# Grouped-query attention scores: the second product of each score tile over 128 stacked rows instead of 64

## The chip, the cores and the metric

The kernel runs on one core of a Trainium2 chip. The metric is the device time of one execution in microseconds. Three runs of the kernel before took 1809.95, 1822.38 and 1826.61 us, median 1822.38 us.

## What is computed

A two-layer trunk works on 256 context tokens and 256 latent tokens of width 1024. Each layer has a feed-forward half step, a mixing sub-layer and a second feed-forward half step. In the mixing sub-layer one input projection is split among three groups: A (a recurrent matrix memory, mLSTM), B (attention with low-rank compression) and C (windowed grouped-query attention). The change touches group C alone, which is cut here to what it needs:

```python
def gqa_branch(...):          # 6 query heads, 2 key heads, head width 64
    q = rms_norm(q, q_norm); k = rms_norm(k, k_norm)      # latent tokens also get a rotary embedding
    s_band = einsum(qb, kb) * C_SCALE                      # latent queries, latent keys within 128 tokens
    s_ctx  = einsum(qb, k_c) * C_SCALE                     # latent queries, all context keys
    p = softmax(concat([s_sink, s_ctx, s_band]))           # a learned sink logit per head
    o = p[ctx] @ v_c + p[band] @ v_band
    # where need_ctx (layer 0 only): the same for the 256 context queries over the context keys, without a band
```

## The kernel before, in words

All weights and activations are fp32. A large product is made as three products of rounded halves: the rounded high part (type fp32r) of each operand, and the rest (the low part). `mm3` (L234) issues high by high, low by high and high by low into one PSUM tile.

The scores of group C do the same with two products, by stacking. `u_q` (L908) writes the query transposed and twice: `twice` (L870) transposes a tile that holds each head's 64 columns two times, so that partitions 0 to 63 and 64 to 127 of the PSUM tile both hold the head. L937 rounds all 128 partitions into `qTC`, and L938 replaces partitions 64 to 127 by what the rounding took off. So one stationary operand of 128 rows holds the query's high part on top and its low part below. `u_k2` (L874) does it for the key: L897 writes the rounded high part on all 128 partitions (`kh`, the first half of `kTC`), and L898 writes what the rounding took off, the low part `kl`, on partitions 0 to 63 alone.

`attend` (L600) makes a tile of 128 queries by `nk` keys for one head (`nk` is 256 in the context stream s=0, 512 in the latent stream s=1). For C the list `prods` (L612) has two products, issued at L614 through `mm` (L231, so every one of them stands under line L232 in the profile, as `sc<-big,w`): the stacked query (128 rows) by `kh`, then the query's upper 64 rows by `kl`. In the latent stream a third product adds the mask (L617, `sc<-maskn,ident`). Then come the row maximum (L625, VectorE), the exponential (L630, ScalarE), the normalisation (L639 or L641), the transposes (L647, TensorE), their copies (L653) and, for two heads together, the product with the values (L661, TensorE, 64 columns of the array each).

There are 36 such tiles in an execution: 12 in the context stream and 12 in the latent stream of layer 0, and 12 in the latent stream of layer 1 (there the context stream is no longer needed). They are not issued in one piece. `mix` (L1161) makes a list of units of work (projections, tiles of B and C, heads of the mLSTM), sorts them by the table `PLAN`, and `run` (L189) steps several of them in turn, so that a tile's steps lie between steps of other units. The framework's scheduler then sets the final order of the instructions of each engine. Each engine runs its own instructions in order and waits at an instruction whose input is not there.

In the layer-0 mix the C tiles run from 536 us to 638 us of the span, in the layer-1 mix from 1519 us to 1573 us. Behind each mix come the output projection (`u_wout`, L1132) and the next feed-forward step.

Of the kernel before, what the change touches and what calls it, by code (L numbers as in the profile page):

```python
# [10 lines left out]
F32 = mybir.dt.float32  # L11
F32R = mybir.dt.float32r
AF = mybir.ActivationFunctionType
ALU = mybir.AluOpType
# [21 lines left out]
def dper(nj):  # L36
    return {2: 4, 3: 2, 4: 2}.get(nj, 1)


# PLAN: order of the units of work of a mix layer, as (first place, step) per group of units.  # L40
# CFG: units taken up per round, units under way at once.  CHP: halves of a weight chunk whose low part Pool makes.
# OPT: engine of a copy or product where it is not the usual one.  BANK, BANKS: PSUM pool by use, and the exceptions.
# MODS: tiles of the next norm made after each column tile of the last group.
PLAN = [
# [11 lines left out]
CFG = [(2, 9), (1, 10)]  # L56
CHP = [
    {"k1": 1, "cq": 1, "o": 1, "k2": 0, "v": 1, "q1": 1, "q2": 1},
    {"k1": 1, "cq": 0, "o": 1, "k2": 0, "v": 0, "q1": 0, "q2": 1},
]  # L60
# [10 lines left out]
BANK = {"k1tr": "tr", "pk": "sc", "pvv": "sc", "cqtr": "tr", "pq": "sc", "k2tr": "tr", "qtr": "tr", "gtr": "tr",  # L71
# [3 lines left out]
BANKS = [  # L75
    {"k1tr": "sc", "C": "ps", "hT": "hold"},
    {"ms": "ps", "ftr": "sc", "hT": "sc"},
    {},
]
MODS = {0: (0, 0, 0, 2, 1, 1, 0, 0), 2: (0, 0, 0, 1, 1, 1, 1, 1), 3: (0, 0, 0, 2, 1, 1, 0, 0)}  # L80


def group(key):
    if isinstance(key, str):
        return key
    if key[0] in "BC":
        return f"{key[0]}{key[1]}{key[2]}"
    if key[0] in ("m", "w", "fin"):
        return f"{key[0]}{key[1]}"
    if key[0] in ("k1", "k2"):  # L90
        return f"{key[0]}{key[1] // 2}"
    return key[0]
# [46 lines left out]
class Builder:  # L139
# [734 lines left out]
    def u_k2(self, l, tt, getps):  # L874
        nc = self.nc
        self.phase = f"K2_{l}"
        lat = 1 if tt >= 2 else 0
        u = slice(tt * P, (tt + 1) * P)
        ps = getps()
        yield  # L880
        self.phase = f"K2_{l}"
        self.cp("VC", self.VC[:, tt, :], ps[:, P:2 * P])
        qk = self.a2([P, 2, 64])
        self.cp("k2", qk, ps[:, 0:P].rearrange("p (a b) -> p a b", a=2))
        qd = self.a2([P, 2, 2, 64])
        yield from self.qknorm(qk, 2, 64, None if lat else qd)
        if lat:
            self.rope(qk, 2, 32, self.tabs_c[tt - 2], 1, qd)
        yield
        self.phase = f"K2_{l}"  # L890
        tr = self.ps((P, 2, P), "k2tr")
        self.twice(tr, qd)
        yield
        self.phase = f"K2_{l}"
        g = self.ones if lat else self.gcol[:, 8:9]
        kh, kl = self.kTC
        self.cp("kh", kh[:, :, u], tr, g)  # L897
        nc.vector.scalar_tensor_tensor(kl[0:64, :, u], tr[0:64], g[0:64], kh.bitcast(F32)[0:64, :, u],  # L898
                                       op0=ALU.mult, op1=ALU.subtract)

    def u_v(self, l, tt, getps):
        self.phase = f"v_{l}"
# [258 lines left out]
    def mix(self, l, need, pre, nxt):  # L1161
        nc = self.nc
# [42 lines left out]
        units = k1[:2] + [("n1", self.u_norm(n1), set())] + k2[:2] + k1[2:] + k2[2:]  # L1205
# [10 lines left out]
        def att(kind, s, hp):  # L1216
            if kind == "B":
                heads = (2 * hp, 2 * hp + 1)
                t = self.attend(f"attB{l}{s}", s, heads, lambda hd, tt: [self.qTB[:, hd, tt * P:(tt + 1) * P]],
                                lambda hd, nk: [self.kTB[:, hd, 0:nk]],  # L1220
                                lambda kt, hd: self.VB[:, kt, hd * 64:hd * 64 + 64], self.y[2 + hp])
                kn, qn = "k1", "cq"
            else:
                def qT(hd, tt):
                    q = self.qTC[hd % 3][:, hd // 3, tt * P:(tt + 1) * P]
                    return q, q[0:64]

                def kT(hd, nk):
                    return self.kTC[0][:, hd // 3, 0:nk], self.kTC[1][0:64, hd // 3, 0:nk]

                t = self.attend(f"attC{l}{s}", s, (hp, hp + 3), qT, kT,
                                lambda kt, hd: self.VC[:, kt, 64 * (hd // 3):64 * (hd // 3) + 64],
                                self.y[5 + hp], masked=True, sink=self.sink)
                kn, qn = "k2", "q1" if hp < 2 else "q2"
            return [((kind, s, hp, k), g, {(kn, tt) for tt in range(2 * s + 2)} | {(qn, 2 * s + k % 2)})
                    for k, g in enumerate(t)]
# [8 lines left out]
        for s in streams:  # L1245
            tiles = [t for u in (("C", 0), ("B", 2), ("C", 1), ("C", 2)) for t in att(u[0], s, u[1])]
# [24 lines left out]
        for u in units:  # L1271
            g = group(u[0])
# [162 lines left out]
```

## Time and profile before

| what | value |
|---|---|
| median of three runs | 1822.38 us |
| the three runs | 1809.95, 1822.38, 1826.61 us |
| profiled execution, span from first to last instruction | 1810.0 us |
| mean granted TensorE clock of the profiled execution | 0.989 |

The profiled execution's span of 1810.0 us is as long as the shortest of the three runs (1809.95 us) and 12.4 us shorter than their median. In the rows below PE is TensorE's matmul, PEld its weight load, DVE VectorE, ACT ScalarE, POOL GpSimd. A matmul's row gives its start and how long it took. Matmuls are pipelined: a row begins while the one before it still drains, so what a matmul costs a busy TensorE is the distance from the end of the one before to its own end, and not its own length. In the shape of a matmul, `64*128 64x512` is a stationary operand of 64 rows and 128 columns and a moving operand of 64 rows and 512 columns.

### The profile page before, as it was taken

The numbers are of one execution on the slowest core, as the hardware profiler recorded it, in microseconds if no ns is written. First come the engines' busy times: TensorE is split into PE (matmuls) and PEld (weight loads), VectorE is DVE, ScalarE is ACT, GpSimd is POOL, SyncE is SP. The second block draws the span as 40 slices with busy tenths as digits, with TensorE's granted clock in tenths as the row PEclk, the third lists the DMA queues.
The fourth block names the chain that finished last, engine by engine and source line by source line (L and its number), as shares of the span: only waits on it lengthen the run. The fifth ranks groups of instructions, "written<-read, shape, count | busy, mean of one in ns | idle before, by whom it ended". The sixth has DMA issues, their size and how long they took to land. (4 is left out here: it accounts for less than half of the span.)

```text
span 1810.0 us, 27331 instructions
## 1 busy us (share of the span) xinstructions
PE 1763.1 (97%) x10098; PEld 1500.9 (83%) x10098; DVE 1235.3 (68%) x2795; ACT 704.3 (39%) x1334; POOL 353.9 (20%) x364
## 2 busy tenths in 40 slices
PE   7999999999999999999999999999999999999999
PEld 5787888889876789888888898888888886699998
DVE  4799698947777766986853469885334788645555
ACT  3422222235565554322322352222222665544443
POOL 2320221035354572000000030000000555340000
PEclk9999999999998999999999999999999999899999
DMA  8656455622110136564533346654223231035654
GB/s 329 206 173 226 148 187 185 210 91 102 36 36 24 48 113 202 189 218 145 199 111 93 119 137 209 212 161 148 79 80 119 68 118 48 12 117 168 205 158 146
DMA packets 99591, 252.35 MB, mean 139 GB/s; under 512 B 12289, under 2 KB 16769, under 8 KB 98433
## 3 DMA queue, kind: packets, MB, share of 16 engines
q1 hardware_dynamic: 99456, 250.60, 42.5%
q8 instruction: 79, 1.29, 0.3%
q14 instruction: 56, 0.45, 0.1%
HBM read 249.51 MB, written 1.05 MB: 138 GB/s over the span
## 5 line engine op out<-in xcount | busy, mean ns | idle before, releaser
L243 ACT ACTIVATE w<-raw 128x1024 fp32r<-128x1024 f32 (+2 forms) x366 | 344.6, 943 | 550.1 <-PE ps L232 277.6
L247 DVE TENSOR_TENSOR w<-raw,w 128x1024 fp32r<-128x1024 f32 (+1 forms) x310 | 333.1, 1075 | 188.0 <-ACT w L243 186.4
L232 PE MATMUL sc<-h,w 128*128 128x512 f32 (+1 forms) x1152 | 303.8, 373 | 0.2 <-DVE h L380 0.2
L232 PE MATMUL tr<-h,w 128*128 128x512 f32 (+1 forms) x1128 | 295.6, 372 | 1.2 <-ACT h L379 0.8
L232 PE MATMUL sc<-big,w 128*128 128x256 f32 (+3 forms) x1200 | 275.4, 337 | 1.7 <-ACT big L379 1.1
L245 POOL TENSOR_TENSOR w<-raw,w 128x1024 fp32r<-128x1024 f32 (+2 forms) x56 | 138.5, 2475 | 652.8 <-ACT w L243 638.5
L232 PE MATMUL ps<-h,w 128*128 128x256 f32 (+1 forms) x1680 | 259.8, 314 | 2.3 <-DVE x L429 2.0
L232 PEld LDWEIGHTS ps<-h,w 128*128 128x128 f32 x1680 | 236.0, 190 | 23.1 <-DVE x L429 2.6
L232 PE MATMUL ps<-big,w 128*128 128x512 f32 (+1 forms) x1152 | 247.3, 374 | 7.8 <-DVE x L429 4.9
L232 PEld LDWEIGHTS ps<-big,w 128*128 128x128 f32 x1152 | 205.3, 189 | 48.0 <-DVE x L429 6.1
L232 PE MATMUL tr<-big,w 128*128 128x256 f32 (+1 forms) x1128 | 243.7, 327 | 0.0
L232 PEld LDWEIGHTS sc<-h,w 128*128 128x128 f32 x1152 | 207.1, 189 | 39.6 <-issue 1.6
L232 PEld LDWEIGHTS tr<-h,w 128*128 128x128 f32 x1128 | 202.9, 189 | 38.5 <-ACT h L379 1.0
L232 PEld LDWEIGHTS sc<-big,w 128*128 128x128 f32 (+1 forms) x1200 | 197.0, 192 | 30.4 <-issue 9.1
L232 PEld LDWEIGHTS tr<-big,w 128*128 128x128 f32 x1128 | 183.0, 192 | 17.8
L345 DVE CUSTOM_DVE_ANT_0 a<-a,a 128x512 f32<-128x512 f32 x256 | 190.3, 743 | 4.3
L345 DVE CUSTOM_DVE_ANT_0 hold<-a,a 128x512 f32<-128x512 f32 x256 | 182.2, 712 | 11.4 <-DMA a<-ada_t 11.2
L232 PE MATMUL ps<-w,h 128*128 128x256 f32 (+1 forms) x1152 | 164.6, 296 | 5.0 <-ACT h L868 2.5
L232 PEld LDWEIGHTS ps<-w,h 128*128 128x128 f32 x1152 | 148.3, 192 | 11.6 <-ACT h L868 2.7
L429 DVE SCALAR_TENSOR_TENSOR x<-ps,gate,x 128x256 f32<-128x256 f32 x192 | 87.3, 480 | 94.5 <-PE ps L232 94.2
L460 DVE TENSOR_TENSOR a<-a,tr 128x512 f32<-128x512 f32 (+1 forms) x90 | 54.3, 603 | 141.6 <-PE tr L232 70.4
L459 ACT ACTIVATE a<-sc 128x512 f32<-128x512 f32 (+1 forms) x91 | 48.3, 531 | 259.7 <-PE sc L232 245.1
(249 smaller groups left out, 1587.1 us busy)
## 6 DMA issues: line engine op xcount, KB each, us to landing
raw<-wi SPq DMA_DIRECT2D x176, 512.0 KB, 4.2
a<-ada_t SPq DMA_DIRECT2D x256, 256.0 KB, 4.7
raw<-wo SPq DMA_DIRECT2D x128, 320.0 KB, 3.0
raw<-w_out SPq DMA_DIRECT2D x24, 512.0 KB, 3.4
big<-ada_s SPq DMA_DIRECT2D x8, 1024.0 KB, 10.9
raw<-wo SPq DMA_DIRECT2D x8, 512.0 KB, 3.7
raw<-win_q SPq DMA_DIRECT2D x8, 512.0 KB, 3.8
a<-crow SPq DMA_DIRECT2D x12, 256.0 KB, 5.7
```

The lines of the kernel that those rows point to most:

```text
L232: self.nc.tensor.matmul(out, lhsT, rhs, start=start, stop=stop)
L243: nc.scalar.activation(h, raw, AF.Copy)
L245: nc.gpsimd.tensor_tensor(l, raw, h.bitcast(F32), op=ALU.subtract)
L247: nc.vector.tensor_tensor(l, raw, h.bitcast(F32), op=ALU.subtract)
L345: nc.vector.tensor_tensor_reduce(out=w if s else junk, in0=w, in1=self.cb[s, hf], scale=1.0, scalar=0.0, op0=ALU.mult, op1=ALU.add, accum_ ...
L429: self.nc.vector.scalar_tensor_tensor(xs, ps, self.gate[l][:, s, i, d:d + 1], xs, op0=ALU.mult, op1=ALU.add)
L459: nc.scalar.activation(sg, pg, AF.Silu)
L460: nc.vector.tensor_tensor(sg, sg, pu, op=ALU.mult)
```

## The change

The low part of the key is written on all 128 partitions, and the second product takes the whole stacked query (128 rows) and the low part of the key on 128 rows. It adds one small term, low by low, to the scores.

```diff
         kh, kl = self.kTC
         self.cp("kh", kh[:, :, u], tr, g)
-        nc.vector.scalar_tensor_tensor(kl[0:64, :, u], tr[0:64], g[0:64], kh.bitcast(F32)[0:64, :, u],
-                                       op0=ALU.mult, op1=ALU.subtract)
+        nc.vector.scalar_tensor_tensor(kl[:, :, u], tr, g, kh.bitcast(F32)[:, :, u], op0=ALU.mult, op1=ALU.subtract)
...
                 def qT(hd, tt):
                     q = self.qTC[hd % 3][:, hd // 3, tt * P:(tt + 1) * P]
-                    return q, q[0:64]
+                    return q, q
 
                 def kT(hd, nk):
-                    return self.kTC[0][:, hd // 3, 0:nk], self.kTC[1][0:64, hd // 3, 0:nk]
+                    return self.kTC[0][:, hd // 3, 0:nk], self.kTC[1][:, hd // 3, 0:nk]
```

Comments above `PLAN` are dropped as well. No instruction is added, removed or moved: each engine has the same instructions in the same order before and after, the DMA queues too. What differs is the shape of 36 matmuls with their weight loads (64 rows become 128) and of eight VectorE instructions of L898 (64 partitions become 128).

## Rows read from the trace of the kernel before

**Rows 1.** The profile page: busy us of each engine, share of the span, instructions.
```profile
PE 1763.1 (97%) x10098; PEld 1500.9 (83%) x10098; DVE 1235.3 (68%) x2795; ACT 704.3 (39%) x1334; POOL 353.9 (20%) x364
```

**Rows 2.** Busy time by stretch, in us; the first line names the columns.
```profile
core 0: us, PE busy (x) PEld busy (x) DVE busy (x) ACT busy (x) POOL busy (x), PEclk, DMA share, GB/s
537.00:552.00 15.00, 12.76 (x93) 10.37 (x94) 11.60 (x26) 8.64 (x28) 8.03 (x8) 1.00 0.15 40
553.52:563.76 10.24, 10.24 (x37) 6.98 (x36) 6.09 (x24) 4.80 (x16) 3.21 (x10) 0.50 0.01 2
564.00:640.00 76.00, 76.00 (x486) 54.55 (x486) 57.68 (x196) 45.74 (x143) 39.32 (x64) 1.00 0.11 36
1548.00:1573.00 25.00, 24.65 (x102) 15.77 (x101) 15.60 (x55) 12.71 (x39) 5.91 (x12) 0.80 0.01 1
```

**Rows 3.** What TensorE waited for, us in total, times, longest: 530:645, then 1500:1585.
```profile
PE sc L1052 <- DVE big L221: 2.2, 1, 2.2
...
PE ps L661 <- DVE a L221: 1.1, 3, 0.6
```

**Rows 4.** The chain that ended last, within 1515:1590: start us, us, what.
```profile
1519.77 0.93 PE sc L232 x3
...
1523.05 3.41 DVE a L1020 x4
...
1567.71 2.09 PE sc L232 x6
...
1573.95 1.48 DVE sa L636
```

**Rows 5.** Groups by line and shape: the 64-row products.
```profile
L232 PE MATMUL sc<-big,w 64*128 64x512 f32 x24 | 12.2, 510 | 0.0
L232 PE MATMUL sc<-big,w 64*128 64x256 f32 x12 | 4.8, 398 | 0.0
```

**Rows 6.** Timeline of TensorE at one latent tile: start us, us, what.
```profile
584.65 0.47 PE L232 MATMUL sc<-big,w 128*128 128x512 f32 x1
...
585.06 0.50 PE L232 MATMUL sc<-big,w 64*128 64x512 f32 x1
...
585.49 0.33 PE L232 MATMUL sc<-maskn,ident 128*128 128x128 f32 x1
```

**Rows 7.** Timeline of TensorE: full products behind one another.
```profile
120.22 0.84 PE L232 MATMUL tr<-h,w 128*128 128x512 f32 x3
120.90 0.84 PE L232 MATMUL sc<-h,w 128*128 128x512 f32 x3
...
665.79 5.88 PE L232 MATMUL ps<-h,w 128*128 128x256 f32 x47
...
545.93 0.28 PE L232 MATMUL ps<-w,h 128*128 128x256 f32 x1
546.05 0.60 PE L647 MATMUL tr<-ident,a 128*128 128x128 f32 x4
```

**Rows 8.** Timeline of TensorE at two context tiles, the first and the seventh.
```profile
536.87 0.38 PE L232 MATMUL sc<-big,w 64*128 64x256 f32 x1
537.18 0.44 PE L647 MATMUL tr<-ident,a 128*128 128x128 f32 x2
...
577.45 0.36 PE L232 MATMUL sc<-big,w 128*128 128x256 f32 x1
577.74 0.38 PE L232 MATMUL sc<-big,w 64*128 64x256 f32 x1
```

**Rows 9.** Groups by line and shape: VectorE's writes of the transposed key.
```profile
L898 DVE SCALAR_TENSOR_TENSOR big<-tr,gcol,big 64x256 fp32r<-64x256 f32 x4 | 1.9, 468 | 0.0
L223 DVE TENSOR_SCALAR big<-tr,gcol 128x256 fp32r<-128x256 f32 x2 | 0.9, 470 | 0.0
```

**Rows 10.** Timeline of TensorE: a 32-row product behind a full one.
```profile
1549.17 0.33 PE L232 MATMUL sc<-maskn,ident 128*128 128x128 f32 x1
1549.43 0.71 PE L1086 MATMUL sc<-C,big 32*128 32x130 f32 x4
```

## The prediction

> **What bounds the kernel now.** I read the page first: TensorE is busy for 97% of the span [rows 1]. That is a mean, so the next view is the busy time by stretch, over the places where the C tiles run. From 564 to 640 us, which holds 20 of the 24 C tiles of layer 0, TensorE is busy for 76.00 of 76.00 us while VectorE has 57.68 and ScalarE 45.74 [rows 2]. There the time is TensorE's: what it no longer does, the stretch no longer has. Ahead of it, from 537 to 552 us, TensorE has 12.76 of 15.00 us [rows 2]; the view of waits puts its one long wait there, 2.2 us for a copy of VectorE (L221) [rows 3], and in the timeline this ends at 551.8 us. In layer 1 the chain of work that ended last can be followed: it goes through C products, leaves them for VectorE (L1020, 3.41 us from 1523.05), comes back, and leaves them again for VectorE behind the six products at 1567.71 [rows 4]. So layer 1 is bound by TensorE in turn with VectorE.
>
> **What the 64-row product costs.** There are 24 of 512 columns and 12 of 256 [rows 5]. A matmul's price to a busy TensorE is the distance between ends. In the latent tile at 584.65 us the first product ends at 585.12, the 64-row one at 585.56, the mask product at 585.82 [rows 6]: 0.44 and 0.26 us, 0.70 together. Full products behind one another have another pace. Two groups of three with 512 columns start 0.68 us apart, 0.227 each; 47 with 256 columns take 5.88 us, 0.12 each; four of 128 columns behind a 256-column one end at 546.65 after 546.21, 0.11 each [rows 7]. So a full second product and the mask behind it should cost 0.227 + 0.11 = 0.34 us, and a latent tile saves 0.70 - 0.34 = 0.36 us. The clock was at its full level in all these rows.
>
> A context tile: the first product ends at 577.81, the 64-row one at 578.12, 0.31 us against 0.12, which saves 0.19. Behind it, at the first such tile, two transposes end 0.37 us after the 64-row product (537.62 against 537.25) instead of 2 x 0.11, which saves 0.15 more [rows 8]. I read the twelve context tiles in the timeline: behind ten stands a full product, which I value at this 0.15; behind two stands a product of 64 columns or 32 rows, which pays its own entry in any case, so nothing is saved there.
>
> Sum on TensorE: 24 x 0.36 = 8.6, 12 x 0.19 = 2.3, 10 x 0.15 = 1.5, together 12.4 us.
>
> Why should the extra time hang on the number of rows? The second product also has a new weight load and adds into the PSUM tile of the first. But so do the products in rows 7, each with its own weights into a tile they share in turn, and they run at 0.227 us. And the extra shows at another partial shape: four 32-row products of 130 columns behind a full one end 0.64 us after it (1550.14 against 1549.50) [rows 10], where four 128-column ones at 0.11 would take 0.44. TensorEngine Tiling (Array Packing), section Key Properties, of the Trainium skill says it as a rule: changing the tiling mode drains the array. These rows agree with it; the page has no price, and the sum goes by the rows.
>
> A rule of the Trainium skill speaks against the change. TensorE: Matmul & The Clock Gate, section LDWEIGHTS (loading the stationary operand), says that a weight load takes its time by columns and not by contraction rows; its table in Why this matters for your kernels adds that a single 32-row matmul takes as long as a 128-row one. By that the product itself gains nothing, and the sum would be 0. It is the first rival below.
>
> **What of it reaches the end.** Three context tiles (at 537, 539 and 543 us) lie ahead of the 2.2 us wait for VectorE; TensorE only comes to that wait earlier, so 3 x 0.34 = 1.0 us is lost. In layer 1 the chain passes through eight of the twelve tiles, from 1519.77 to 1567.71 [rows 4]; the other four run beside VectorE, so 4 x 0.36 = 1.4 us is lost. The remaining 10.0 us lie where TensorE is the bound. A TensorE that runs some 7 us ahead in layer 0 will meet waits that do not show now. They cost between nothing and all of layer 0's share, 7 us; the nearest rows are the waits of layer 1, 1.1 us in three [rows 3], and I take 1.0 us. That leaves 9.0 us.
>
> **The other edit.** Eight L898 instructions write 128 partitions instead of 64. A 64-partition one took 468 ns, and a VectorE instruction on 128 partitions with the same source tile and the same 256 elements 470 ns [rows 9]: 8 x 2 ns, which is nothing. If time did go by partitions it would be 8 x 0.47 = 3.8 us more on VectorE, ahead of the C tiles, and the score tiles that wait for the key would be late by 0.5 us at each layer's last one. I keep that bound, as 1 us, in the range.
>
> **The sum.** The profiled execution of 1810.0 us would become 1801.0. It is as fast as the fastest of the three runs; their median is 12.4 us above it. I take the 9.0 us off the median: 1822.4 - 9.0 = 1813.4 us. The three runs lie 0.9% apart, so about 1% is what a measurement of this kernel can tell from no change.
>
> **Rivals.**
>
> First, the change doesn't do what it says: the extra 0.2 and 0.15 us belong to something else in the pair of products, and a full second product costs as much as the 64-row one. For it speaks only that no row shows a C tile with a full second product; against it speak rows 7 and 10. The time is then 1822.4.
>
> Second, the drains go but layer 0 gives the gain back. VectorE has 57.68 of 76 us of its own there and the tiles go through ScalarE, VectorE or GpSimd and TensorE in turn; a TensorE ahead of them waits at the transposes (L647) and value products (L661). Then only layer 1's eight tiles count, 2.9 us, with 1 us of layer 0: 1818.5. Against it: not one wait of TensorE over 0.6 us after 552 us in that mix shows now.
>
> Third, the granted clock. Two stretches of 10.24 us among the C tiles ran at 0.50, the 1.2 GHz level; in the first, from 553.52, TensorE was busy for all of it [rows 2], so each cost about 5.1 us. If fuller products keep the clock up there, 10.2 us come on top of the 9.0: 1803.2. Against it: ahead of the first stretch stands the 2.2 us wait, which the change doesn't shorten.
>
> Fourth, the side of slower: that wait begins 1.0 us earlier and so lasts 3.2 us. The clock fell at 553.52, behind just this idle time. If it stays at the lower level for three more lengths like that, to about 594 us, that costs 15.4 us against 9.0: 1822.4 + 6.4 = 1828.8. It decides from two more lengths on (10.2 against 9.0). Against it: the level came back at 563.76 while TensorE was busy throughout, and it is no less busy afterwards.
>
> **Chances.** The forecast 0.57, with a range of its own of 1807 to 1819 (1810.0 if all 12.4 us count, less 3 us of scatter between runs; 1819 if no more than a third of the 10.0 us counts). No gain 0.10. Given back 0.16. Clock stays up 0.10. Clock falls longer 0.07. The range from 1803 to 1824 holds the forecast, the first two rivals and half of the third. Faster by over 1% means under 1804.2: half of the third rival and a tail of the forecast by scatter, 0.12. Slower by over 1%, over 1840.6, would take five lengths of the fourth rival or more: 0.03. Within 1%: 0.85.
>
> **What would show it.** In the profile of the changed kernel the rows `64*128` of `sc<-big,w` are gone. The second product of a latent tile ends 0.23 us after the first and the mask 0.11 us after that; of a context tile 0.12 us. TensorE's busy time in the layer-0 mix falls by about 7 us with the stretch itself, and its wait before L1052 near 551 us grows from 2.2 to about 3.2 us. If the ends still lie 0.43 us apart, the first rival holds; if they close up and waits before L647 and L661 grow by several us, the second. A time above 1824 with those ends closed up would say that the clock, or something I have not seen, outweighs the drains.

## The result, and the profile after

The changed kernel takes 1794.4 us (median of four runs, 1794.11 to 1796.5) against 1817.34 us of the kernel before in the same comparison: a ratio of 0.9883, 95% interval 0.9834 to 0.9932, so some 23 us less. Timed again beside two of the experiments it took 1794.27 us, ratio 0.9861 (0.9815 to 0.9907). Slow runs, those over 1.5% above the fastest of the same kernel, are left out of all medians, ranges and ratios here. The forecast was 1813.4 us in a range from 1803 to 1824: the direction was right, the size was not, and the time lies below the range.

The profiled executions are 1810.0 us before and 1792.4 us after, 17.6 us apart. The page of the changed kernel, as in [rows 1], with the granted clock by slices below it:

```profile
span 1792.4 us, 27331 instructions
...
PE 1743.0 (97%) x10098; PEld 1494.7 (83%) x10098; DVE 1235.2 (69%) x2795; ACT 703.5 (39%) x1334; POOL 355.3 (20%) x364
...
PEclk9999999999998999999999999999999999999999
```

TensorE is busy 20.1 us less; VectorE, ScalarE and GpSimd are busy as long as before. The row of the clock has one slice under 9, the thirteenth. In the kernel before there are two, the thirteenth and the thirty-fifth, which lies in layer 1's mix:

```profile
PEclk9999999999998999999999999999999999899999
```

The timeline of TensorE in the changed kernel, at the latent tile of [rows 6] and at the seventh context tile of [rows 8]:

```profile
573.75 0.39 PE L232 MATMUL sc<-big,w 128*128 128x256 f32 x1
...
573.75 0.51 PE L232 MATMUL sc<-big,w 128*128 128x256 f32 x2
...
580.51 0.47 PE L232 MATMUL sc<-big,w 128*128 128x512 f32 x1
...
580.83 0.40 PE L232 MATMUL sc<-big,w 128*128 128x512 f32 x1
581.06 0.23 PE L232 MATMUL sc<-maskn,ident 128*128 128x128 f32 x1
```

In the latent tile the ends are 580.98, 581.23 and 581.29: the second product comes 0.25 us after the first instead of 0.44, and the mask 0.06 us after that instead of 0.26. In the context tile the second product ends at 574.26, 0.12 us after the first (574.14), instead of 0.31. The other tiles at full clock agree: before, the second product of a latent tile ends 0.43 us and its mask another 0.26 us later, after, 0.23 and 0.06 us. So the price per tile was read right.

Now the two stretches of C tiles as wholes, each from the end of the first tile's first product to the end of the last tile's mask. First the kernel before, whose stretches of [rows 2] were cut otherwise (the columns are those of [rows 2]), then the changed kernel:

```profile
536.94:638.63 101.69, 99.45 (x613) 72.12 (x613) 75.25 (x247) 59.29 (x188) 49.97 (x82) 0.95 0.11 37
1520.00:1573.17 53.17, 52.06 (x285) 33.50 (x285) 36.08 (x111) 27.76 (x85) 18.90 (x33) 0.87 0.10 31
```

```profile
536.13:629.81 93.68, 90.90 (x612) 70.62 (x611) 74.53 (x245) 57.99 (x187) 50.10 (x81) 0.95 0.12 36
1511.93:1555.71 43.78, 41.41 (x284) 29.46 (x284) 35.61 (x110) 27.06 (x83) 18.84 (x32) 1.00 0.11 37
...
552.54:562.78 10.24, 10.24 (x41) 6.84 (x40) 5.75 (x22) 4.65 (x15) 3.31 (x10) 0.50 0.01 2
```

Layer 0 is 101.69 - 93.68 = 8.0 us shorter at the same mean clock of 0.95; its stretch at the 1.2 GHz level is still there, 10.24 us long. Layer 1 is 53.17 - 43.78 = 9.4 us shorter, and there the granted clock rose from 0.87 to 1.00. At 0.87 a stretch of 53.17 us has lost 0.13 x 53.17 = 6.9 us to the lower level, so 2.5 us of the 9.4 are the drains; this is an estimate, which takes TensorE, busy for 52.06 us of it, as the bound all along. Together 8.0 + 9.4 = 17.4 of the 17.6 us: by this estimate 10.5 us are drains, 6.9 us are clock.

What TensorE waited for in the changed kernel, from 520 to 640 us (as in [rows 3]):

```profile
PE sc L1051 <- DVE big L221: 2.4, 1, 2.4
PE ps L232 <- POOL a L1070: 0.4, 1, 0.4
```

The wait for VectorE's copy grew by 0.2 us, and one wait of 0.4 us is new.

### The profile page after: what moved, and what is told of

Same layout as the page of the kernel before. It is cut to its first block, busy times and chain, and to the rows that moved or that the text cites. A ratio compares the mean times of both kernels' runs of the same rounds, so it can differ in the third digit from the quotient of the medians.

```text
span 1792.4 us, 27331 instructions
## 1 busy us (share of the span) xinstructions
PE 1743.0 (97%) x10098; PEld 1494.7 (83%) x10098; DVE 1235.2 (69%) x2795; ACT 703.5 (39%) x1334; POOL 355.3 (20%) x364
## 5 line engine op out<-in xcount | busy, mean ns | idle before, releaser
L232 PE MATMUL sc<-big,w 128*128 128x256 f32 (+1 forms) x1200 | 266.9, 332 | 1.7 <-ACT big L379 1.1
L232 PEld LDWEIGHTS sc<-big,w 128*128 128x128 f32 x1200 | 193.8, 192 | 22.7 <-ACT big L379 1.3
L345 DVE CUSTOM_DVE_ANT_0 hold<-a,a 128x512 f32<-128x512 f32 x256 | 182.0, 711 | 11.7 <-DMA a<-ada_t 11.5
```

The source lines that it names most:

```text
L232: self.nc.tensor.matmul(out, lhsT, rhs, start=start, stop=stop)
L345: nc.vector.tensor_tensor_reduce(out=w if s else junk, in0=w, in1=self.cb[s, hf], scale=1.0, scalar=0.0, op0=ALU.mult, op1=ALU.add, accum_ ...
```

## The experiments

Three questions were open: whether the edit of VectorE or the products did it, what exactly about 64 rows costs, and why the granted clock changed. The table gives the medians; each ratio is to runs of the kernel before on the same chip. The kernel before has a median clock of 0.985 in these runs, with single runs from 0.978 to 0.993, and times from 1805.2 to 1828.5 us that follow the clock.

| kernel | median us | ratio (95%) | granted clock, median (range) |
|---|---|---|---|
| changed kernel, first comparison | 1794.4 | 0.9883 (0.9834 to 0.9932) | 0.992 (0.992) |
| changed kernel, again | 1794.27 | 0.9861 (0.9815 to 0.9907) | 0.991 (0.989 to 0.992) |
| wide write, 64-row product | 1816.9 | 1.0015 (0.9971 to 1.0059) | 0.985 (0.977 to 0.993) |
| layer 0 alone | 1804.0 | 0.9958 (0.9929 to 0.9987) | 0.990 (0.981 to 0.991) |
| layer 1 alone | 1806.3 | 0.9931 (0.9897 to 0.9965) | 0.989 (0.986 to 0.991) |
| 96 rows | 1795.9 | 0.9902 (0.9869 to 0.9936) | 0.992 (0.988 to 0.993) |
| mask over 64 rows | 1808.0 | 0.9933 (0.9905 to 0.9960) | 0.989 (0.986 to 0.990) |
| zeros in the lower half | 1794.7 | 0.9864 (0.9818 to 0.9910) | 0.992 (0.991 to 0.992) |
| value products pinned | 1803.6 | 0.9928 (0.9885 to 0.9972) | 0.988 (0.984 to 0.991) |
| full filler | 1805.8 | 0.9947 (0.9917 to 0.9978) | 0.991 (0.989 to 0.994) |

Edits are shown against the changed kernel. In all but the last two rows of the table the scheduler left the order of the instructions as in the changed kernel (the zeros add two instructions of ScalarE); in the last two it moved some.

**The write alone.**

```diff
-                    return q, q
+                    return q, q[0:64]
...
-                    return self.kTC[0][:, hd // 3, 0:nk], self.kTC[1][:, hd // 3, 0:nk]
+                    return self.kTC[0][:, hd // 3, 0:nk], self.kTC[1][0:64, hd // 3, 0:nk]
```

> The key's low half is written on 128 partitions, the second product stays at 64 rows. Theory (the time is saved by the products, not by VectorE's edit): as the kernel before, a ratio of 0.997 to 1.003, ends of the 64-row products still 0.43 us behind the first one. Rival (the wider write saves or costs time): a ratio under 0.995 or over 1.005.

The ratio is 1.0015: the wider write does nothing, and all of the change is in the products. Its profile shows something else. It issues the same matmuls as the kernel before, and the 64-row products end 0.43 us behind the first ones as they do there, but it was granted another clock. Layer 0's stretch of C tiles, and two pieces of it:

```profile
536.26:643.80 107.54, 105.30 (x612) 75.80 (x613) 75.40 (x247) 59.48 (x188) 49.97 (x82) 0.89 0.11 35
552.60:562.84 10.24, 10.24 (x38) 7.05 (x36) 5.96 (x24) 4.76 (x17) 3.19 (x9) 0.50 0.01 2
576.50:590.15 13.65, 13.65 (x45) 9.00 (x44) 6.04 (x27) 4.84 (x19) 2.53 (x7) 0.50 0.01 2
```

Behind the stretch at 552.60 that every profile here has, a second one stands at 576.50, 13.65 us long, in which TensorE never stood idle. It lies among the context tiles, and it costs 107.54 - 101.69 = 5.9 us against the profiled execution of the kernel before. This execution, 1817.6 us, stands near the median of its kernel (1816.9). So the scatter of the kernel before was time at the lower level, and part of it arose at the very tiles that the change touches.

**One layer at a time.**

```diff
-                    return q, q
+                    r = P if l == 0 else 64
+                    return q, q[0:r]
...
-                    return self.kTC[0][:, hd // 3, 0:nk], self.kTC[1][:, hd // 3, 0:nk]
+                    r = P if l == 0 else 64
+                    return self.kTC[0][:, hd // 3, 0:nk], self.kTC[1][0:r, hd // 3, 0:nk]
```

(For layer 1 alone the condition is `l == 1`.)

> Full rows in layer 0 alone (24 of 36 tiles). Theory of the drains: 7 to 8 us of the span go, all of them between 536 and 640 us of the span. On the granted clock in layer 1: if the 64-row products themselves let the clock fall there, the lower level comes back in layer 1 (over 10 us of it between the first C tile and the end of that mix) and the time is about 1802; if it was only a matter of where in time the mix comes, it may stay up as in the changed kernel and the time is about 1798.

> Full rows in layer 1 alone (12 tiles). Theory of the drains: 3 to 4 us of the span go, between 1519 and 1575 us. On the granted clock: if the 64-row products let it fall, layer 1 has no lower level among its C tiles, 6 to 7 us more go, and the time is 10 us under the kernel before's; if the place in time decides, the lower level is there as before and only 3 to 4 us go.

Against 1815.6 us, the median of the kernel before beside them, the two gains are 11.6 and 9.3 us by the medians, 7.6 and 12.5 us by the ratios of the table; they add up to 20 or 21 us. The kernel with 96 rows, which ran beside these two, gains 19.7 us by the medians, and the whole change brought 22.9 us in the first comparison. So the gains of the layers add up within the spread, but how they share it is known to 5 or 6 us only, the width of each interval to either side. The stretches of C tiles of both layers, first with layer 0 alone full, then with layer 1 alone full:

```profile
537.52:631.22 93.70, 90.91 (x613) 70.66 (x611) 74.55 (x245) 57.94 (x187) 49.96 (x81) 0.95 0.12 37
1513.36:1566.49 53.13, 52.03 (x284) 33.31 (x285) 36.06 (x111) 27.76 (x85) 18.86 (x33) 0.87 0.10 31
```

```profile
536.90:640.01 103.11, 100.87 (x613) 73.00 (x613) 75.31 (x247) 59.47 (x188) 49.96 (x82) 0.93 0.11 37
1521.36:1565.15 43.79, 41.41 (x284) 29.46 (x284) 35.62 (x110) 27.02 (x83) 18.79 (x32) 1.00 0.11 37
```

This tells the place in time from the products. With layer 0 alone, layer 1 begins 6.6 us earlier than in the kernel before and is still 53.13 us long at a clock of 0.87. With layer 1 alone, it begins 1.4 us later and is 43.79 us long at 1.00, as in the changed kernel. With the instructions in this order, the lower level of layer 1 goes with the 64-row products and not with the moment at which the stage begins. The two forecasts of the first expectation lay too close together to be told apart by the time (1802 and 1798; the median is 1804.0), the rows above decide; for the second the time is 9.3 us (medians) or 12.5 us (ratio) under the kernel before's, around the 10 us of the first branch.

How the 64-row products do it is not shown. The lower level does not stand at them alone, as three stretches of the kernel before show:

```profile
1525.50:1543.38 17.88, 17.12 (x126) 10.78 (x126) 13.96 (x42) 9.25 (x29) 7.41 (x16) 1.00 0.19 60
1543.38:1546.80 3.42, 3.42 (x18) 1.72 (x16) 1.63 (x6) 0.00 (x0) 1.38 (x3) 0.50 0.00 0
1550.21:1560.45 10.24, 10.24 (x31) 6.62 (x31) 5.05 (x20) 4.85 (x16) 2.80 (x6) 0.50 0.00 0
```

The fourth 64-row product of layer 1 ends at 1525.91 and the fifth begins at 1548.74. Between them the clock stays at 1.00 for 17 us, and then falls amid value products (L661). The changed kernel has the same products there and keeps its clock.

**96 rows.**

```diff
-                    return q, q
+                    return q, q[0:96]
...
-                    return self.kTC[0][:, hd // 3, 0:nk], self.kTC[1][:, hd // 3, 0:nk]
+                    return self.kTC[0][:, hd // 3, 0:nk], self.kTC[1][0:96, hd // 3, 0:nk]
```

> The second product takes 96 of the 128 rows (it leaves out half of the low by low term). Theory (the array changes to a form of 64 rows and back, and 96 rows need the full form): as the changed kernel, 1794 us, second product ends 0.23 us after the first of 512 columns. Rival (any second product with other rows than the first pays): as the kernel before, ends 0.43 us apart, 1810 us or more.

```profile
580.90 0.48 PE L232 MATMUL sc<-big,w 128*128 128x512 f32 x1
...
581.21 0.39 PE L232 MATMUL sc<-big,w 96*128 96x512 f32 x1
...
581.44 0.22 PE L232 MATMUL sc<-maskn,ident 128*128 128x128 f32 x1
```

The ends are 581.38, 581.60 and 581.66, and the time is the changed kernel's within 2 us. A second product that uses other rows than the first pays nothing at 96 rows, and pays 0.2 us at 64. That is what a change of the array's form to 64 rows and back would do. TensorEngine Tiling (Array Packing), section Available Configurations, of the Trainium skill lists forms of 128, 64 and 32 rows and none of 96; this run agrees, at the full pace of 0.22 us.

**The mask over 64 rows.** This leaves the mask off for 64 of the 128 queries of each latent tile.

```diff
-                self.mm(sc[:, mk * P:(mk + 1) * P], self.identr, self.maskn[:, qi, :], False, True)
+                self.mm(sc[:, mk * P:(mk + 1) * P], self.identr[0:64], self.maskn[0:64, qi, :], False, True)
```

> The changed kernel, with the mask product of the 24 latent tiles over 64 rows instead of 128 (it leaves the mask off for half of the queries). All score products are full, and each latent tile again has one change to a 64-row form and back, now over 128 columns only. Theory (the change of form costs, whatever its columns): ends of the mask product about 0.3 us behind the score product instead of 0.11, and 0.15 us more behind it, 24 x 0.35 = 8 us over the changed kernel, and the lower granted clock among the C tiles comes back in some runs, so that they spread by 10 us or more; about 1804 to 1812. Rival (the 512 columns over 64 rows were what cost): at most 2 us over the changed kernel, and the clock stays at 0.992.

The timeline at the first latent tile:

```profile
581.19 0.40 PE L232 MATMUL sc<-big,w 128*128 128x512 f32 x1
...
581.52 0.32 PE L232 MATMUL sc<-maskn,ident 64*128 64x128 f32 x1
```

The mask ends 0.25 us after the score product (581.84 against 581.59) instead of 0.06. The stretch of layer 1's C tiles:

```profile
1516.56:1570.00 53.44, 52.26 (x283) 34.05 (x283) 36.38 (x111) 27.76 (x84) 18.91 (x33) 0.84 0.09 30
```

The time is 13.7 us over the changed kernel's, more than the 8 us of the drains, since layer 1 is back at 53.44 us with a clock of 0.84. The runs spread by 9 us, a little less than expected. The 512 columns over 64 rows are not needed for any of it: 24 products of 64 rows and 128 columns do it.

**Zeros in the lower half.** The second product has 128 rows, the lower 64 rows of the key's low part are zeros, so its values are those of the kernel before.

```diff
         self.kTC = bg4[:, 0], bg4[:, 1]
+        nc.scalar.activation(bg4[64:128, 1], self.ones[64:128].unsqueeze(2).to_broadcast([64, 2, NT]), AF.Copy, scale=0.0)
...
-        nc.vector.scalar_tensor_tensor(kl[:, :, u], tr, g, kh.bitcast(F32)[:, :, u], op0=ALU.mult, op1=ALU.subtract)
+        nc.vector.scalar_tensor_tensor(kl[0:64, :, u], tr[0:64], g[0:64], kh.bitcast(F32)[0:64, :, u],
+                                       op0=ALU.mult, op1=ALU.subtract)
```

> The changed kernel with zeros in the lower half of the key's low part: the second product has 128 rows in its shape but only 64 of them carry numbers, as in the kernel before. Theory (shape alone decides): as the changed kernel, 1794 to 1796 us and a clock of 0.992. Rival (the work that the array really does decides on the clock): ends as in the changed kernel, 10 us under the kernel before at the same clock, but a clock that falls as before in some runs, 1797 to 1815.

> The changed kernel once more, beside these two on one chip: 1794 to 1797 us, clock 0.991 to 0.993 in nearly every run.

1794.7 against 1794.27 us for the changed kernel beside it, and a clock of 0.991 or 0.992 in seven of the eight runs of the two (0.989 in the other). What the rows carry plays no part that these runs show, in the time or in the clock.

**A filler without a change of form.** The mask is left off, and the key's high part is added to the scores twice instead.

```diff
-                self.mm(sc[:, mk * P:(mk + 1) * P], self.identr, self.maskn[:, qi, :], False, True)
+                self.mm(sc, self.identr, prods[0][1], False, False)
+                self.mm(sc, self.identr, prods[0][1], False, True)
```

> The changed kernel, with the mask product of the 24 latent tiles replaced by two full products of 512 columns (the identity by the key's high part, which leaves the mask off and adds the key to the scores). Each latent tile costs TensorE 2 x 0.227 - 0.11 = 0.34 us more, as much as the mask over 64 rows did, but with no change of the array's form. Theory (it is the changes of form that let the granted clock fall): 24 x 0.34 = 8 us over the changed kernel, about 1802, and a clock of 0.991 to 0.992 with runs within 3 us of one another. Rival (any longer C stage lets it fall): a clock of 0.986 to 0.990 and 1805 to 1812.

The stretch around layer 1's C tiles in its profile:

```profile
1510.00:1565.00 55.00, 53.34 (x336) 37.85 (x335) 38.69 (x122) 32.60 (x97) 23.17 (x38) 0.99 0.09 30
```

Every latent tile is longer for TensorE by about as much as with the 64-row mask, and the clock stays at 0.99 there, where the 64-row mask had 0.84. The profiled execution is the fastest of the ten, so the other runs matter too: their clocks are 0.989 to 0.994, with the 64-row mask 0.986 to 0.990. The time, 1805.8 us, is 11.5 us over the changed kernel's instead of the 8 us expected and lies in the rival's range, and the runs spread by 3.8 us rather than 3. But the six runs of 1805.8 us and more have clocks of 0.990 to 0.992, as the profiled one has (0.991), so the other 3 us are not clock. The scheduler had moved some instructions for the two longer products; where these 3 us are stays open. For the clock: a longer stage of full products did not lower it, 64-row products in their place did.

**The value products in fewer groups.** The products with the values (L661) use 64 columns and also change the form; the scheduler had split them into 32 groups.

```diff
-                        nc.tensor.matmul(pv[64 * b2:64 * b2 + 64, :], V(kt, h2), pts[b2][kt // 2][:, kt % 2, :],
-                                         start=kt == 0, stop=kt == nkt - 1, tile_position=(0, 64 * b2))
+                        ins = nc.tensor.matmul(pv[64 * b2:64 * b2 + 64, :], V(kt, h2), pts[b2][kt // 2][:, kt % 2, :],
+                                               start=kt == 0, stop=kt == nkt - 1, tile_position=(0, 64 * b2))
+                        self.tc.keep_in_program_order(ins)
```

> The changed kernel, with the value products (L661, 64 columns of the array) pinned in the order in which they are written, so that TensorE meets them in 21 groups instead of 32. Theory (each change of the array's form costs some 0.25 us in and 0.15 us out, here too): 11 groups fewer, 11 x 0.4 = 4 us under the changed kernel, 1790 us, if no new waits come of it. Rival (pinning makes TensorE wait for the softmax of a tile where it had other work): waits before L661 of some us each, 1800 us or more.

What TensorE waited for in it, from 530 to 650 us:

```profile
PE ps L232 <- POOL a L1071: 2.7, 1, 2.7
PE sc L1052 <- DVE big L221: 2.4, 1, 2.4
PE sc L232 <- ACT a L630: 1.2, 2, 0.7
PE tr L873 <- DVE sa L636: 1.0, 1, 1.0
```

The waits came, though elsewhere than the rival said: TensorE waits 2.7 us for GpSimd, 1.2 us for the exponential and 1.0 us for a sum. With 1803.6 us at a clock of 0.988 the version is 9 us slower than the changed kernel. But waits are not all of it: 0.988 against 0.992 is some 7 us more at the lower level (0.004 x 1800, an estimate), and the profiled execution has 0.984. In layer 1 its clock fell here:

```profile
1535.82:1546.06 10.24, 10.00 (x41) 7.20 (x41) 5.34 (x19) 2.41 (x7) 3.22 (x10) 0.50 0.00 0
```

All score products of this version are full, and its value products come in fewer groups. So the lower level can come back in layer 1 without 64-row products and with fewer changes of form (24 in its stage of layer 1 against 30 in the changed kernel's, counted by the shapes); the stretch holds 32-row products and value products, as do the stretches in the kernel before. How the 9 us are shared between waits and clock, and whether the fewer groups saved their 4 us, these runs do not tell. None of these kernels beats the changed one.

## Why the prediction was wrong

**The price of a tile was right.** The prediction put a latent tile's saving at 0.36 us, as 0.2 at the second product and 0.15 behind it; the ends in the changed kernel give 0.19 at the product and 0.20 at the mask, 0.39 us for the tile where both are counted.

**What reaches the end was a little too small, 9.0 instead of 10.5 us.** Two of its steps failed. The 1.0 us of the three tiles ahead of the wait was not lost. I had taken VectorE's copy for a fixed date, but VectorE itself had waited for TensorE. VectorE in the kernel before, then in the changed kernel:

```profile
542.68 0.76 DVE L221 COPY a<-tr 128x256 f32<-128x256 f32 x2 [2.12 <-PE tr L647]
...
551.48 0.29 DVE L221 COPY big<-tr 128x128 f32<-128x128 f32 x1
```

```profile
541.14 0.76 DVE L221 COPY a<-tr 128x256 f32<-128x256 f32 x2 [1.75 <-PE tr L647]
...
549.75 0.29 DVE L221 COPY big<-tr 128x128 f32<-128x128 f32 x1
```

Its last long idle time ahead of that copy ends with transposes of TensorE, which stand behind the first two of these tiles. The copy came 1.7 us earlier, 0.8 us of it because the whole stretch began earlier, and the wait grew by 0.2 us and not by 1.0. And the 1.0 us for new waits in layer 0 did not come: 0.4 us did. Layer 1 gave 2.5 us of drains where I had 2.9. Runs at about the same granted clock put the drains higher still: at 0.991 to 0.993 the kernel before took 1805.8 to 1810.5 us, at 0.991 and 0.992 the changed kernel 1793.7 to 1796.5, some 13 us apart, which is near the 12.4 us of the prediction's sum on TensorE.

**The step that failed is "I take the 9.0 us off the median".** It treated the distance between the profiled execution and the median, and the 0.9% between the three runs, as scatter that the change leaves alone. It was time at the 1.2 GHz level: the runs of the kernel before have clocks from 0.978 to 0.993 and their times go with them, while the changed kernel has 0.992 in all four runs of its first comparison and lies within 2.4 us. At the medians (0.985 and 0.992) the lower level took 0.015 x 1816 = 27 us of the kernel before and 0.008 x 1793 = 14 us of the changed one; the difference, 13 us, and the 10.5 us of drains make 23.5, against the measured 22.9. These are estimates: by the runs at the same clock it is 13 us of drains and 10 us of clock. Either way 10 us or more of the change are clock, a term that the sum put at nothing.

**The third rival named this and was given 0.10.** Its price per stretch, 5.1 us for 10.24, was about right (13.65 us cost 5.9 us in the write alone), and so was its argument that the stretch behind the 2.2 us wait would stay: it is still there at 552.54, as long as before. Of its two stretches the other one went, that from 1550.21, and with it a shorter one from 1543.38, so that layer 1's mean clock of 0.87 became 1.00. Its gain of 19.2 us came near the measured 22.9, in part by luck: it counted the stretch at 553.52, which stayed, and left out the stretches that the profiled execution of the kernel before happened not to have, such as the one at 576.50 in the experiment with the write alone. That three runs lay 17 us apart, and that the profiled one was as fast as the fastest of them, stood in the prediction; the question to ask there was whether the profile shows a mild case of a cost that the median holds in full.

**The other rivals.** That the change does nothing fell with the ends of the products. Weight loads of the kernel before (`sc<-big,w`, the score products among others), 128 rows and 64:

```profile
L232 PEld LDWEIGHTS sc<-big,w 128*128 128x128 f32 x1164 | 190.2, 192 | 22.3 <-issue 2.4 <-ACT big L379 1.3 <-ACT a L1062 0.7
L232 PEld LDWEIGHTS sc<-big,w 64*128 64x128 f32 x36 | 6.8, 188 | 8.1 <-issue 6.7
```

The rule in TensorE: Matmul & The Clock Gate, section LDWEIGHTS (loading the stationary operand), of the Trainium skill, that the rows of a weight load don't matter, agrees with this trace for the load itself, 188 ns against 192. What failed is what the first rival made of it: its load does not set the price of a 64-row product in a stream of full ones, where the measured 0.44 us became 0.25 with 128 rows. The rule of TensorEngine Tiling (Array Packing), section Key Properties, of the Trainium skill, that a change of form drains the array, agrees with the ends in these runs, 0.43 us at 64 rows and 0.23 us at 96 and 128. Given back as waits: no, 0.4 us. The clock lower for longer: the opposite happened.

## What to carry to other kernels

In a stream of full 128-row products, a product of 64 rows cost 0.35 to 0.4 us more than a full one here: 0.2 going in, at 128, 256 and 512 columns alike, and 0.15 to 0.2 behind it. If its operands can be had on 96 or 128 partitions, fill them, with zeros if need be. Read the scatter between runs before taking a gain off the median: where it follows the granted clock, ask which products stand in the stretches at the lower clock, for a change to them can also be paid in clock. A wait is a fixed date only if the chain behind it does not begin at what you shorten.

## What the runs showed of the hardware

The granted clock fell to its 1.2 GHz level in stretches in which TensorE was never idle by the profile (13.65 of 13.65 us busy at 576.50), amid products of 64 rows, 32 rows or 64 columns. In layer 1 it stayed up with the same stage lengthened by full products (0.99); with the lower half of the rows zero, and with 96 rows, the whole execution had 0.992. It fell again with 24 products of 64 rows over 128 columns each (0.84 in layer 1's stretch), and, with full score products, when the value products were pinned (0.50 from 1535.82 to 1546.06). What the chip counts there is not settled by these runs: the drain at a change of form and the half-filled array come together in each of them, and in layer 1 of the kernel before the clock fell 17 us behind the 64-row product ahead of it (at 1543.38). Nor is it settled why the stretch at 552.54 stays: it stands behind the 2.4 us wait and beside 32-row products, and neither was taken away. The mLSTM's 32-row products were not made full in any run.
